# First MLP's down projection as 16 pairs of seven-product blocks, rows finished by accumulating transfers, first key and query products in row groups

## The chip, the core and the metric

The kernel runs on one core of a Trainium2 chip. The metric is device time in microseconds (us) of one execution; the time before is the median of three runs. The profile is of one more execution of the same program. TensorE is PE in the profile, VectorE is DVE, ScalarE is ACT, GpSimd is POOL, SyncE is SP.

## The reference: what is computed

A trunk of two layers works on 1024 prompt tokens and 8 sample tokens, so on T = 1032 columns of width 1024. Layer 0 mixes tokens with a recurrent block, layer 1 with sliding-window attention; after each mixer comes a squared-ReLU MLP. All is float32.

```python
def sq_relu_mlp(x, w_up, w_down):
    return jnp.square(jax.nn.relu(x @ w_up)) @ w_down      # 1024 -> 4096 -> 1024

yp = yp + mp                                               # mixer's output
yp = yp + sq_relu_mlp(rms_norm(yp, norm_mlp_g[layer]), w_up[layer], w_down[layer])
# layer 1 then begins with
h = rms_norm(yp, norm_mix_g[1]); q, k, v = split(h @ w_qkv); q, k normed per head
```

The change lies at the end of layer 0's MLP and at the beginning of layer 1's attention.

## The kernel before, in words

**Number format.** Each float32 operand is split into a high part (`hi`, rounded by an ACT cast) and a low part (`lo`, what is left, by a DVE subtraction). A product is three passes: hi·hi, hi·lo, lo·hi, that is three matmuls for each block of 128 rows of the contraction.

**Seven-product blocks.** The two MLPs are computed in the manner of Strassen and Winograd. Two 128-row tiles of the hidden width are a pair (16 pairs in all), and two 128-row tiles of the output are a block `q`. A block takes seven products (`i` = 1 to 7 in `BY`) of sums of weight quarters (`S1` to `S4`, built by DVE) with sums of token halves (`B11`, `T1` and so on). A product of one pair is three matmuls of 512 columns (i = 1, 2, 4) or six of 260 (i = 3, 5, 6, 7). The contraction is over several pairs at once, a chunk. `steady` writes the order of the products by hand: within a block 1, 6, 2, 7, 4, 5, 3, with the next block's product 1 before this block's product 3; in the last block (`FINAL`) 1, 6, 7, 4, 5, 2, 3. `e` and `o` are the two rows of output tiles of a block; product 5 completes `o`, and product 3 is accumulated in the same PSUM tile (`z["d"]`) after DVE has read product 5 out of it, and completes `e`.

**Down projection of layer 0.** The up projection writes the sums of the hidden tokens to DRAM (`hsum`). The down projection runs over chunks of pairs; for each chunk it makes four blocks (eight output rows), loading `tl` tiles from `hsum` and splitting them (ACT L467, DVE L468). Before, layer 0 has 14 pairs in this form, in chunks of 3, 3, 3, 3 and 2. Finished rows of the first four chunks are added to the residual in DRAM by an accumulating transfer of POOL (L773: `acc[m] += t`). For the last chunk, the transfer goes the other way (L782: `t += acc[m]`), and the row stays in SBUF. The other two pairs are four plain hidden tiles (`hid`, `hdh`/`hdl`), and `down_steps` multiplies them in the ordinary way: for each third of the columns (344 columns) and each of eight rows twelve matmuls, then DVE adds the product to the row (L384), ACT squares it for the norm (L290) and makes `hh` (L390), DVE makes `hl` (L391). After each third the squares of eight rows, summed by DVE, go through a matmul with ones (L302, `tokens`). Layer 1's down projection has all 16 pairs as blocks, in chunks of 4, 3, 3, 3 and 3.

**First products of the attention.** `proj_many` makes the first key and first query tile (`k0`, `q0`) third by third: 24 matmuls of a key third, 24 of a query third. Each key third is then normed by a serial chain: ACT squares it (L851) and copies it (L852), a matmul with the head mask sums the squares (L858), DVE and ACT find the factor (L859, L314 to L316, L317, L319), DVE multiplies (L926), and ACT and DVE split the result (L869, L870). There is one PSUM bank for the sums (`bN`). `proj_steps` then makes the second key tile (`k1`, 72 matmuls, L943), with three such chains more. `v_proj` (216 matmuls of 256 columns, L973) accumulates four pairs of token blocks in two banks (`bS`), and the eight samples in `bT`. ACT reads these banks out (L983), with a scale per token `rt`, which `by_token` issues behind the last key chain. After that comes the second query tile.

**What sets the order.** The code is written in program order, and a scheduler then moves instructions in each engine's queue by priority and by its estimate of when they are ready; on the chip every queue runs in its order. Loads of weights pass through two `raw` tiles of the pool `rp` (SP issues them), and a `raw` tile comes free when ACT and DVE have split it (L183, L184).

Of the kernel before, what the change touches and what calls it, by code (L numbers as in the profile page):

```python
# [16 lines left out]
P = 128  # L17
# [13 lines left out]
CHUNKS = [[range(0, 3), range(3, 6), range(6, 9), range(9, 12), range(12, 14)],  # L31
          [range(0, 4), range(4, 7), range(7, 10), range(10, 13), range(13, 16)]]
NSP = [c[-1][-1] + 1 for c in CHUNKS]
RQ = [6 * P, 8 * P]
NRAW = [4, 3]
# [30 lines left out]
def trunk(ctx: ExitStack, tc: tile.TileContext, I, O):  # L66
# [103 lines left out]
    def fetch(n):  # L170
        while len(raws) < min(n, len(units)):
            name, _, src, _ = units[len(raws)]
            if name[:2] == "dn":
                raws.append(small["pool"].tile([P, RQ[int(name[2])]], F32, tag="Q", name=nm("raw")))
            else:
                raws.append(R("raw"))
            sp.dma_start(raws[-1][:, 0:src.shape[1]], src)
# [23 lines left out]
    for layer in range(2):  # L201
        add_units(f"up{layer}", I["w_up"][layer], 2 * NPAIR, lambda j: None)
        for b in range(4 * len(CHUNKS[layer])):
            for j in range(2):
                units.append((f"dn{layer}", 2 * b + j, I[f"w_dn{layer}"][2 * b + j][:, 0:2 * P * len(CHUNKS[layer][b // 4])], None))
# [8 lines left out]
    def ensure(k):  # L214
        while nloaded[0] <= min(k, len(units) - 1):
            n, j, _, alloc = units[nloaded[0]]
            fetch(nloaded[0] + (NRAW[int(n[2])] if n[:2] == "dn" else 2))
# [131 lines left out]
    def tokens(ssq, c):  # L349
# [4 lines left out]
        ssq.total(ps)  # L354
# [17 lines left out]

    def down_steps(w, srcs, xs, gname, hs, after=None, col=lambda m, k: k * P, early=0):
        for c in range(NCH):
            ssq = SumSq(plain=True)
            held = []
            if c == 0 and early:
                held = banks3("P")
                for m in range(3):
                    yield from mm_steps([held[m]], w(m), srcs, [c], col=lambda k: col(m, k), ks=range(early))  # L380
            for m in range(M8):
                o, ks = (held[m], range(early, len(srcs))) if m < len(held) else (B("P" if held and m == 3 else None)[:, :CH], None)
                yield from mm_steps([o], w(m), srcs, [c], col=lambda k: col(m, k), ks=ks)
                dve.tensor_tensor(xs[m][:, cs(c)], o, xs[m][:, cs(c)], ALU.add)  # L384
                if after:
                    after(m, c)
                x, (hi, lo), g = xs[m][:, cs(c)], hs[m], V(gname, m)
                with tc.high_priority():
                    ssq.add(x, m)
                act.activation(r_(hi[:, cs(c)]), x, AF.Copy, scale=g)  # L390
                dve.scalar_tensor_tensor(r_(lo[:, cs(c)]), x, g, hi[:, cs(c)], ALU.mult, ALU.subtract)  # L391
            if c == 0:
                last["c0"] = last["sq"]
            tokens(ssq, c)

# [74 lines left out]
    class TokenOps:  # L472
# [43 lines left out]
        def T1(self, e, o, j):  # L516
# [6 lines left out]
    LAST = {"tile": (24, 25, 26, 27), "split tile": (28, 31, 34, 38),  # L523
            "weights": (14, 15, 23, 24), "split weights": (19, 22, 53)}
# [19 lines left out]
    PROGS = [UP + steady("dn", range(4 * len(c))) for c in CHUNKS]  # L544
# [4 lines left out]
    class PairWeights:  # L549
        def __init__(self, layer):  # L550
            self.layer = layer
            self.prog, self.chunks = PROGS[layer], CHUNKS[layer]
# [83 lines left out]
    class Ahead:  # L636
        def __init__(self, layer):
            self.sums = hsum[layer]
            self.chunks = CHUNKS[layer]
# [3 lines left out]
            self.pooled = layer  # L643
            self.lag = {0: 4, 1: 4} if layer else {0: 4}
# [7 lines left out]
        def split(self, step):  # L652
            with tc.issue_after(last["copy"]):
                while self.raw and self.raw[0][0] <= step - self.lag.get(self.raw[0][1], 5):
                    _, c, name, t = self.raw.pop(0)
                    pooled = self.pooled and c == 0 and len(self.ops[c][name]) in ()
                    self.ops[c][name].append(op_at(*t, pool if pooled else dve))
# [24 lines left out]
    xd = []  # L682

    def mlp_products(layer, tok, pw, r, spill, acc, gnext, after):
        ahead = Ahead(layer)
        chunks, nsp = CHUNKS[layer], NSP[layer]
        final = None if gnext else 4 * len(chunks) - 1
        hs, raw = [], []
        ws, wraw = [], []
        xs = xd  # L690
        xs[:] = [None] * M8
# [5 lines left out]
        def last_tile(k):  # L697
            lo, hi = A("hdl"), A("hdh")
            pool.dma_start(lo, hid[layer][k])
            return hi, lo  # L700

        def last_weights(j):
            t = R("raw")
            sp.dma_start(t[:, 0:D], I[f"w_dn{layer}"][8 * len(chunks) + j])
            return t

        for n, (kind, q, i) in enumerate(PROGS[layer]):
# [7 lines left out]
            if (kind, q, i) == ("up", NU, 4):  # L715
                swap_small(f"q{layer}", NRAW[layer])
            wt = pw.take(n)
            first = up and q < 2
            if i == 1:
                st[q] = {"z": ZB(), "e": spare("he") if not up and q in range(2 if gnext else 1, 12 if gnext else final - 1) else A("he"), "o": A("ho")}  # L720
# [12 lines left out]
            with tc.high_priority():  # L733
                if i == 1:
                    last["copy"] = act.copy(e0, d).ins  # L735
                elif i == 6 and not first:
# [4 lines left out]
                    if not up and q == final:  # L741
# [10 lines left out]
                elif i == 2 and not first:  # L752
                    last["copy"] = act.copy(e0, d).ins  # L753
                    if not up and q == final:
# [8 lines left out]
            for ready in done:  # L763
                t = z[ready]
                if up:
                    dve.scalar_tensor_tensor(t, t, 0.0, r, ALU.min, ALU.mult)
                    act.activation(t, t, AF.Square)
                    if q >= nsp:
                        act.dma_start(hid[layer][2 * (q - nsp) + (ready == "o")], t)
# [4 lines left out]
                elif q == final:  # L774
# [6 lines left out]
                else:  # L781
                    pool.dma_start(t, acc[m], accum_op=ALU.add)  # L782
# [4 lines left out]
            if "e" in done:  # L787
                if up and q < nsp:
# [9 lines left out]
            elif not up:  # L798
                c, k = divmod(n - NUP, 28)
                ahead.split(n)  # L800
                if final:
# [22 lines left out]
        if final:  # L824
            return
# [826 lines left out]
```

## Time and profile before

| | |
|---|---|
| median of 3 runs | 1953.07 us (1952.73 to 1954.8) |
| profiled execution | 1954.17 us, of which the span from the first to the last instruction is 1952.4 us |
| PE, PEld, DVE, ACT, POOL busy | 99%, 93%, 76%, 52%, 18% of the span |
| down blocks of layer 0 (14 pairs) | 649.03 to 928.27 us |
| `down_steps` | 928.27 to 975.39 us |
| first key product to the first matmul of the second query tile | 975.39 to 1040.56 us |
| down blocks of layer 1 (16 pairs) | 1628.82 to 1947.03 us |

The stages are read from the timeline of PE: the start of the first matmul of each. Busy shares of matmuls are modelled, and a matmul's own duration (282 ns for one of 260 columns) overlaps its neighbours', so the pitch of matmuls is taken from start to start.

### The profile page before, as it was taken

The page shows a single profiled execution, that of the slowest core. Times are in us where ns is not written, and L with a number is a line of the kernel's source. Part 1 is how long each engine was busy: PE and PEld are TensorE (multiplying, and loading weights), DVE is VectorE, ACT ScalarE, POOL GpSimd, SP SyncE. Part 2 cuts the span into 40 slices and gives each one's busy share as a digit, 9 for nine tenths or more (in the row PEclk, how much of TensorE's full clock was granted, in tenths as well). Part 3 has the DMA queues.
Part 4 walks back from the last instruction along what each step waited for, and adds up shares of the span by engine and source line. Part 5 has one row for each costly group of instructions (what it writes and reads, how often), then busy time and mean ns, then how long its engine had stood idle before and what let it go on. Part 6 is the DMA issues. An engine that isn't in the chain of part 4 may idle for free.

```text
span 1952.4 us, 34246 instructions
## 1 busy us (share of the span) xinstructions
PE 1939.8 (99%) x12844; PEld 1806.6 (93%) x12844; DVE 1477.1 (76%) x2715; ACT 1007.5 (52%) x1993; POOL 359.0 (18%) x699
## 2 busy tenths in 40 slices
PE   9999999999999999999999999999999999999998
PEld 9999999999999899999999887999999999999998
DVE  7996747987777888778753778589877779687884
ACT  6585635443434655455554667465444436455552
POOL 1320000000000232322022667000000003223221
PEclk9999999999999999999999999999999999999999
DMA  5111242244445788888453336622443447788877
GB/s 188 40 45 54 80 156 84 100 162 158 142 158 175 230 223 240 215 198 209 137 150 91 110 101 203 211 84 99 163 145 138 163 166 261 211 196 218 237 193 181
DMA packets 115909, 308.17 MB, mean 158 GB/s; under 512 B 17560, under 2 KB 46240, under 8 KB 115744
## 3 DMA queue, kind: packets, MB, share of 16 engines
q0 software_dynamic: 30720, 104.18, 22.2%
q1 hardware_dynamic: 56800, 131.45, 20.5%
q10 hardware_dynamic: 28224, 70.35, 10.0%
q8 instruction: 101, 1.65, 0.4%
q14 instruction: 64, 0.52, 0.1%
HBM read 178.08 MB, written 115.16 MB: 150 GB/s over the span
## 4 chain that ended last, share of the span: by engine, by line
PE 93%; DVE 3%; ACT 2%; issue 1%; DMA 1%; POOL 0%; SPq 0%; DVEq 0%; ACTq 0%
PE bD L613 36%; PE bZ L613 26%; PE bP L244 12%; PE bS L244 7%; PE bT L244 3%; PE bP L943 3%; PE bO L1084 1%; PE bSS L1037 1%; PE bS L973 1%; PE bT L1064 1%; ACT se L1050 1%; DVE op L461 1%; DMA x<-spill 0%; DMA raw<-w_in 0%; DVE wl L184 0%
## 5 line engine op out<-in xcount | busy, mean ns | idle before, releaser
L613 PEld LDWEIGHTS bD<-op,op 128*128 128x128 f32 x3072 | 380.6, 188 | 7.9
L613 PE MATMUL bD<-op,op 128*128 128x260 f32 x3072 | 383.2, 282 | 0.0
L613 PEld LDWEIGHTS bD<-tl,op 128*128 128x128 f32 x2880 | 362.2, 188 | 11.8 <-DVE ho L761 0.3
L613 PE MATMUL bD<-tl,op 128*128 128x260 f32 x2880 | 366.2, 282 | 0.1
L626 POOL DMA_DIRECT2D tl<-hsum x210 | 125.2, 682 | 884.5 <-PE bD L613 783.5
L460 ACT CAST op<-ws 128x512 fp32r<-128x512 f32 (+2 forms) x288 | 158.4, 560 | 248.4 <-DVE ws L581 124.6
L613 PE MATMUL bZ<-op,op 128*128 128x512 f32 x1152 | 282.3, 395 | 0.0
L613 PE MATMUL bZ<-tl,op 128*128 128x512 f32 x1080 | 271.9, 395 | 0.2 <-DVE tl L468 0.2
L613 PEld LDWEIGHTS bZ<-op,op 128*128 128x128 f32 x1152 | 210.5, 188 | 43.9 <-ACT he L747 0.2
L613 PEld LDWEIGHTS bZ<-tl,op 128*128 128x128 f32 x1080 | 194.3, 188 | 37.7 <-DVE tl L468 0.7
L468 DVE TENSOR_TENSOR tl<-tl 128x520 fp32r<-128x520 f32 (+1 forms) x210 | 136.6, 692 | 77.0 <-ACT tl L467 76.9
L460 ACT CAST op<-raw 128x512 fp32r<-128x512 f32 (+2 forms) x216 | 120.8, 561 | 139.1 <-PE bD L613 76.5
L461 DVE TENSOR_TENSOR op<-ws,op 128x512 fp32r<-128x512 f32 (+2 forms) x288 | 171.5, 610 | 8.7 <-ACT op L460 8.5
L461 DVE TENSOR_TENSOR op<-raw,op 128x512 fp32r<-128x512 f32 (+2 forms) x216 | 131.5, 610 | 5.4 <-ACT op L460 4.5
L761 DVE TENSOR_TENSOR ho<-bD,ho 128x520 f32<-128x520 f32 x140 | 97.5, 696 | 37.4 <-PE bD L613 35.0
L467 ACT CAST tl<-tl 128x520 fp32r<-128x520 f32 (+1 forms) x210 | 117.7, 626 | 2.4 <-DMA tl<-hsum 1.0
L184 DVE TENSOR_TENSOR wl<-raw,wh 128x512 fp32r<-128x512 f32 (+1 forms) x76 | 65.7, 885 | 37.6 <-ACT wh L183 20.8
L751 DVE TENSOR_TENSOR ho<-bZ,ho 128x512 f32<-128x512 f32 x72 | 49.5, 687 | 43.7 <-PE bZ L613 43.3
L761 DVE TENSOR_TENSOR he<-bD,he 128x520 f32<-128x520 f32 x71 | 49.4, 696 | 40.9 <-PE bD L613 40.4
L753 ACT COPY he<-bZ 128x512 f32<-128x512 f32 x68 | 39.9, 587 | 78.0 <-PE bZ L613 65.6
L183 ACT CAST wh<-raw 128x512 fp32r<-128x512 f32 (+1 forms) x76 | 56.9, 775 | 41.9 <-PE bT L244 13.9
L735 ACT COPY he<-bZ 128x512 f32<-128x512 f32 x72 | 42.0, 583 | 70.4 <-PE bZ L613 70.3
(371 smaller groups left out, 3811.5 us busy)
## 6 DMA issues: line engine op xcount, KB each, us to landing
raw<-w_up SPq DMA_DIRECT2D x64, 512.0 KB, 3.9
tl<-hsum POOLq DMA_DIRECT2D x120, 260.0 KB, 6.8
raw<-w_dn SPq DMA_DIRECT2D x64, 384.0 KB, 6.2
tl<-hsum POOLq DMA_DIRECT2D x90, 256.0 KB, 6.7
spill<-ho POOLq DMA_DIRECT2D x32, 516.0 KB, 6.8
spill<-he POOLq DMA_DIRECT2D x32, 516.0 KB, 6.2
hsum<-ts ACTq DMA_DIRECT2D x30, 520.0 KB, 4.0
hsum<-ho ACTq DMA_DIRECT2D x30, 516.0 KB, 3.6
```

What stands on the lines that cost most here:

```text
L183: act.copy(r_(hi[:, sl]), raw[:, sl])
L184: eng.tensor_tensor(r_(lo[:, sl]), raw[:, sl], hi[:, sl], ALU.subtract)
L244: pe.matmul(o, lhsT=r_(wt[:, col(k):col(k) + P]), rhs=r_(xt[:, cs(c)]), start=(k == first and a == 0), stop=(k == final and a == 2))
L460: act.copy(r_(hi), x)
L461: dve.tensor_tensor(r_(lo), x, hi, ALU.subtract)
L467: act.copy(r_(hi), lo)
L468: eng.tensor_tensor(r_(lo), lo, hi, ALU.subtract)
L613: pe.matmul(d[:, 512 * b:512 * b + c], lhsT=r_(wt[:, j * P:j * P + P]), rhs=r_(xt[:, c * b:c * b + c]), start=first and j == 0 and a == 0, ...
L626: pool.dma_start(t[:, n:2 * n], src)
L751: dve.tensor_tensor(o0, d, o[:, HP], ALU.add)
L761: last["sum"] = dve.tensor_tensor(t, inner(d), t, ALU.add).ins
L943: pe.matmul(o, lhsT=r_(wt[:, k * P:k * P + P]), rhs=r_(xt[:, cs(c)]), start=(k == 0 and a == 0), stop=(k == M8 - 1 and a == 2))
```

## The change

Layer 0 gets layer 1's plan: all 16 pairs as blocks, chunks of 4, 3, 3, 3 and 3, and three `raw` tiles of down weights in place of four. `down_steps`, the four plain tiles and their weights are gone. The eight rows of the last chunk are finished by accumulating transfers, the last `e` row in two parts. As each row lands, `row(m)` squares it over all 1032 columns (ACT), makes `hh` (ACT) and `hl` (DVE), adds the square to one running sum (DVE) and stores the row (SP). The first key and query products then hold six banks at once and take the rows in three groups: rows 0 to 3, rows 4 and 5, rows 6 and 7. The three matmuls with ones stand between the products of the second group. The six results are read out after the third group.

```diff
-CHUNKS = [[range(0, 3), range(3, 6), range(6, 9), range(9, 12), range(12, 14)],
-          [range(0, 4), range(4, 7), range(7, 10), range(10, 13), range(13, 16)]]
-NRAW = [4, 3]
+CHUNKS = [range(0, 4), range(4, 7), range(7, 10), range(10, 13), range(13, 16)]
+NRAW = 3
...
-    def mlp_products(layer, tok, pw, r, spill, acc, gnext, after):
+    def mlp_products(layer, tok, pw, r, acc, gnext, store):
...
+        def row(m):
+            x, g, s, hi, lo = xs.pop(m), V(gnext, m), A("sq"), A("hh"), A("hl")
+            act.activation(s, x, AF.Square)
+            act.activation(r_(hi), x, AF.Copy, scale=g)
+            sp.dma_start(store[m], x)
+            if sq:
+                dve.tensor_tensor(sq[0], sq[0], s, ALU.add)
+            else:
+                sq.append(s)
+            dve.scalar_tensor_tensor(r_(lo), x, g, hi, ALU.mult, ALU.subtract)
+            hn[m] = (hi, lo)
...
                 elif i == 2 and not first:
                     last["copy"] = act.copy(e0, d).ins
-                    if not up and q == final:
+                    if not up and q == final and gnext:
+                        pool.dma_start(e0, acc[2 * (q % 4)][:, H0], accum_op=ALU.add)
+                    elif not up and q == final:
...
                 else:
-                    pool.dma_start(t, acc[m], accum_op=ALU.add)
+                    sl = slice(HW if q == final and ready == "e" else 0, T)
+                    pool.dma_start(t[:, sl], acc[m][:, sl], accum_op=ALU.add)
...
+                if gnext and c == len(chunks) - 1:
+                    m = 2 * (q % 4) - 2
+                    if i == 7 and m >= 0:
+                        row(m + 1)
+                    if i == 5 and m >= 0:
+                        row(m)
+                    if q == final and i in (2, 5):
+                        ensure(index["k" if i == 2 else "q", 0])
...
-        ws += [split_unit(t, W, dve) for t in wraw]
-        hn = [(A("hh"), A("hl")) for _ in range(M8)] if gnext else None
-        run(down_steps(lambda m: ws, hs, xs, gnext, hn, after=after, col=lambda m, k: m * P, early=2))
-        return hn
+        row(7)
+        row(6)
+        rs["sq"] = sq[0]
+        return [hn[m] for m in range(M8)]
...
-        with tc.issue_after(last["c0"]):
-            wk, wq = unit("k", 0, 1), unit("q", 0, 1)
-        proj_many([wk, wq], hs, lambda i, c, o: q_evac(0, c, o) if i else k_evac(0, c, take_out(o), fx["row"][:, cs(c)]))
+        ws = [unit("k", 0, 0), unit("q", 0, 0)]
+        firsts = [(i, c, B()[:, :CH]) for c in range(NCH) for i in range(2)]
+        for rows in (range(0, 4), range(4, 6), range(6, 8)):
+            for i, c, o in firsts:
+                mm_group([o], ws[i], hs, [c], ks=rows)
+                if rows[-1] == 5 and i:
+                    tokens(rs["sq"][:, cs(c)], c)
+        for i, c, o in firsts:
+            if i:
+                q_evac(0, c, o)
+            else:
+                k_evac(0, c, take_out(o), fx["row"][:, cs(c)])
         run(proj_steps(unit("k", 1, 1), lambda c, o: k_evac(1, c, take_out(o), fx["row"][:, cs(c)]), iter(())))
         by_token()
         v_proj()
```

Three places in the built programs show how queues change. The same code has lower line numbers in the changed kernel: L582 for L613, L715 and L727 for L751 and L761, L819 for L858, L934 for L973.

The first is DVE at the last block of the down projection. Before, after the last product's reading the queue goes on with `down_steps`:

```order
L761 TENSOR_TENSOR ho_9744<-bD_9798,ho_9744 128x520
L751 TENSOR_TENSOR ho_9744<-bZ_9818,ho_9744 128x512
L761 TENSOR_TENSOR ho_9744<-bD_9826,ho_9744 128x520
L761 TENSOR_TENSOR he_9743<-bD_9826,he_9743 128x520
L384 TENSOR_TENSOR he_9377<-bP_9894,he_9377 128x344
```

Now the sum of squares and the low half of row 4 (`sq_10170`, `he_9870`, the row of the block before) stand between the last block's own readings (`ho_10035`, `he_10034`):

```order
L665 TENSOR_TENSOR sq_9813<-sq_9813,sq_10170 128x1032
L715 TENSOR_TENSOR ho_10035<-bZ_10138,ho_10035 128x512
L668 SCALAR_TENSOR_TENSOR hl_10172<-he_9870,vec,hh_10171 128x1032
L727 TENSOR_TENSOR ho_10035<-bD_10149,ho_10035 128x520
L725 TENSOR_TENSOR he_10034<-bD_10149,he_10034 128x260 x2
```

The reading of product 5 (`L727 ho_10035`), which the last product waits for, has moved behind two instructions that wait for a row in flight.

The second is ACT between the first key third's square and the second's. Before (`wh` casts split weights; `bP_10438` and `bS_10530` are key thirds):

```order
L851 ACTIVATE sq_10463<-bP_10438 128x344
L852 COPY x_10464<-bP_10438 128x344
L314 ACTIVATE q_10475<-sq_10463,st 128x344
L315 ACTIVATE r_10474<-q_10475 128x344
L316 ACTIVATE q_10475<-r_10474 128x344
L881 ACTIVATE sq_10520<-bS_10493 128x344
L183 CAST wh_10708<-raw_10430 128x512
L869 CAST hi_10482<-x_10464 128x344
L883 CAST hi_10522<-bS_10493 128x344
L183 CAST wh_10708<-raw_10430 128x512
L183 CAST wh_10886<-raw_10706 128x512 x2
L851 ACTIVATE sq_10555<-bS_10530 128x344
```

Now, from the first third's logarithm on (`bP_10276` is the second key third; `raw_10571` and `raw_10749` are the second value tile's and the second query tile's weights):

```order
L311 ACTIVATE q_10457<-sq_10445,st 128x344
L312 ACTIVATE r_10456<-q_10457 128x344
L180 CAST wh_10751<-raw_10571 128x512
L313 ACTIVATE q_10457<-r_10456 128x344
L180 CAST wh_10751<-raw_10571 128x512
L180 CAST wh_10759<-raw_10749 128x512 x2
L830 CAST hi_10464<-x_10446 128x344
L844 CAST hi_10479<-bP_10275 128x344
L812 ACTIVATE sq_10487<-bP_10276 128x344
```

Four casts of newly loaded weights have moved into the first chain, and the second key third's square stands behind the end of that chain.

The third is PE around the sixth and last key norm (`bN`). Before, it stands in the middle of the first value bank's 48 products:

```order
L973 MATMUL bS_10900<-wh_10886,hh_9892 128x256
L973 MATMUL bS_10900<-wl_10887,hh_9892 128x256
L973 MATMUL bS_10900<-wh_10886,hl_9893 128x256
L858 MATMUL bN_10849<-sq_10845,con 128x344
L973 MATMUL bS_10900<-wh_10708,hh_9878 128x256
```

Now the samples' 24 products (`bT`) follow the first two value banks, and the norm stands among them; `bS_10867` is the third value bank, which takes the place of the first:

```order
L934 MATMUL bT_10972<-wl_10752,hh_10131 8x256
L819 MATMUL bN_10714<-sq_10710,con 128x344
L934 MATMUL bT_10972<-wh_10751,hl_10132 8x256
L934 MATMUL bT_10972<-wh_10751,hh_10241 8x256
L934 MATMUL bT_10972<-wl_10752,hh_10241 8x256
L934 MATMUL bT_10972<-wh_10751,hl_10242 8x256
L934 MATMUL bT_10972<-wh_10751,hh_10233 8x256
L934 MATMUL bT_10972<-wl_10752,hh_10233 8x256
L934 MATMUL bT_10972<-wh_10751,hl_10234 8x256
L934 MATMUL bS_10867<-wh_10573,hh_9862 128x256
```

Between the last norm and the third value bank stand now 7 products, where before stood 72.

More of the change, by code (lines that the diff above doesn't have):

```diff
@@ L353, in tokens @@
         ps = B("N")[:, :CH]
-        ssq.total(ps)
+        pe.matmul(ps, lhsT=ones, rhs=sq, start=True, stop=True)
         act.copy(row[:, cs(c)], ps)
@@ L695, in spare @@
             return R(s)
[L697 to L707, printed above, removed]
+        def row(m):
[9 more added lines that the diff above has]
+            hn[m] = (hi, lo)
+        for n, (kind, q, i) in enumerate(PROG):
             up = kind == "up"
@@ L800, in mlp_products @@
                 ahead.split(n)
[L801 removed]
+                if True:
                     if c == 0 and k in NEXT:
@@ L1498, in ahead, with mlp @@
         return f
-    def mlp(layer, r, spill, gnext, after):
+    def mlp(layer, r, acc, gnext, store):
         swap_banks(f"pu{layer}")
-        return mlp_products(layer, rs.pop("tok"), rs.pop(layer), r, None, spill, gnext, after)
+        return mlp_products(layer, rs.pop("tok"), rs.pop(layer), r, acc, gnext, store)
     r0 = A("rt")
```

101 lines of the change are left out of this document (26 added, 75 removed).

## The prediction, made before the run

> **What bounds the kernel.** I read the page first.
>
> ```profile
> span 1952.4 us, 34246 instructions
> ...
> PE 1939.8 (99%) x12844; PEld 1806.6 (93%) x12844; DVE 1477.1 (76%) x2715; ACT 1007.5 (52%) x1993; POOL 359.0 (18%) x699
> ```
>
> PE bounds it, and hardly ever stands still. So the change is worth what it takes from PE's products, less each new pause of PE. The waits of PE say how little there is now:
>
> ```profile
> PE bO L1084 <- DVE pt L1068: 1.5, 1, 1.5
> ```
>
> That is the longest of all (total, times, longest, in us). Then the table of stretches, for the two down projections and what lies around:
>
> ```profile
> core 0: us, PE busy (x) PEld busy (x) DVE busy (x) ACT busy (x) POOL busy (x), PEclk, DMA share, GB/s
> 649.03:928.27 279.24, 279.01 (x1850) 255.65 (x1849) 225.20 (x427) 150.26 (x293) 77.27 (x118) 1.00 0.83 213
> 928.27:975.39 47.12, 47.12 (x295) 46.20 (x293) 35.59 (x71) 25.66 (x53) 0.88 (x1) 1.00 0.46 132
> 975.39:1040.56 65.17, 64.86 (x448) 61.40 (x447) 27.72 (x57) 30.31 (x70) 14.84 (x29) 1.00 0.48 133
> 1628.82:1947.03 318.21, 318.12 (x2114) 292.10 (x2112) 241.30 (x444) 156.74 (x299) 86.07 (x135) 1.00 0.80 207
> ```
>
> These are layer 0's 14 pairs, `down_steps`, the first key, query and value products, and layer 1's 16 pairs. In each PE is busy nearly all the time.
>
> **Part 1: the products, a gain.** Layer 0 takes on the plan that layer 1 runs already, so the price of 16 pairs stands in the last row: 318.21 us. It replaces 279.24 + 47.12 = 326.36: **-8.15 us**. Of this 1.4 us is no gain, as two matmuls with ones move from `down_steps` into the next stage; I count them there. A check by matmuls:
>
> ```profile
> 1940.47 2.32 PE L613 MATMUL bD<-tl,op 128*128 128x260 f32 x18
> 1942.63 2.25 PE L613 MATMUL bZ<-tl,op 128*128 128x512 f32 x9
> 1944.71 2.32 PE L613 MATMUL bD<-tl,op 128*128 128x260 f32 x18
> ```
>
> ```profile
> 928.43 13.27 PE bP L244 x84
> ...
> 977.92 0.70 PE bN L302 x2
> ```
>
> From start to start a matmul of 260 columns takes 2.16/18 = 0.120 us, one of 512 takes 2.08/9 = 0.231, one of 344 takes 13.27/84 = 0.158. Out go 288 of 344 columns, 45.5 us; in come 2 pairs x 4 blocks x (24 of 260, 9 of 512), 39.7 us: -5.8. The stages give -8.15 + 1.4 = -6.75, as layer 0's blocks run 0.06 us a pair slower than layer 1's. I take the stages and keep -5.8 for the upper end. The other additions (two pairs' sums stored, 14 more `tl` loads, wider weights) hide as in layer 1, whose stretch pauses for 0.1 us.
>
> **Part 2: the finishing of rows, a loss in the last blocks.** `row` puts, per row, two ACT instructions of 1032 columns and two DVE instructions into blocks 17 to 19. In layer 1 nothing of this kind stands there. The prices:
>
> ```profile
> L467 ACT CAST hdh<-hdl x4: 1056/1057/1057, 889.9 to 903.6; 128x1032 fp32r<-128x1032 f32 x4
> L468 DVE TENSOR_TENSOR hdl<-hdl,hdh x4: 1222/1222/1224, 891.0 to 905.0; 128x1032 fp32r<-128x1032 f32 x4
> ```
>
> ```profile
> 924.96 0.69 DVE L751 TENSOR_TENSOR ho<-bZ,ho 128x512 f32<-128x512 f32 x1
> 925.76 0.70 DVE L761 TENSOR_TENSOR ho<-bD,ho 128x520 f32<-128x520 f32 x1
> 928.47 0.70 DVE L761 TENSOR_TENSOR he<-bD,he 128x520 f32<-128x520 f32 x1 [2.01 <-PE bD L613]
> ```
>
> ```profile
> 929.68 0.88 POOL L782 DMA_DIRECT2D he<-spill  x1 [1.84 <-issue]
> ```
>
> ```profile
> DMA to landing us min/median/max: 5.4/6.0/7.2
> ```
>
> The last is the accumulating transfer of a finished row in layer 0. Follow row 4 from the end of block 18's last product. DVE completes it at 0.2 to 0.9; POOL issues at 1.4 (929.68 against 928.47, 1.2 us later); it lands at 7.4; ACT squares it to 8.5. DVE's queue holds the sum of squares there, and behind it, in order, the reading of product 4, row 4's low half, and the reading of product 5: 8.5 + 1.22 + 0.69 + 1.22 + 0.70 = 12.3. The last product accumulates onto product 5's bank, so PE must wait for this; its own five products before end at 3 x 2.16 + 2 x 2.08 = 10.6. PE waits **1.7 us** (1.1 to 2.9 for the landing's ends). Blocks 17 and 18 have the same order with one more product as cover, but also build the next block's weights; I put 0.4 us on each, between 0 and 1 (an estimate from the same rows). Together **+2.5 us**, with ends 0.5 and 5.
>
> Rows 6 and 7 themselves are covered. The last part of row 6 is complete 0.8 us after the last product and lands by about 8; square, sum, high and low halves are done by 12. PE has 72 + 12 matmuls, 13.3 us, before the first matmul with ones, and 19 us before it needs the row.
>
> **Part 3: the key norms, the larger loss.** Before, each of the first three norms stood behind a query third, and its chain ran beside products. Now all six banks end together, so the first chain begins when the last product of `k0` and `q0` is done. A chain step is serial, and this is what the chain of waits shows from one norm to the next:
>
> ```profile
> 1011.47 0.86 PE bN L858 x2
> ...
> 1016.79 0.46 ACT sq L851
> ...
> 1017.29 0.84 PE bN L858 x2
> 1018.14 19.80 PE bS L973 x168
> ```
>
> One norm follows another after 5.82 us at best, because ACT's queue takes the next square only behind the split of this key. A product of 256 columns takes 19.80/168 = 0.118 us. Behind the last norm comes:
>
> ```profile
> 1023.37 0.30 ACT L314 ACTIVATE q<-st,vec 128x9 f32<-128x9 f32 x1 [0.26 <-DMA kh<-hi]
> ...
> 1024.72 0.84 ACT L983 ACTIVATE vt<-bS,st 128x256 f32<-128x256 f32 x2 [0.56 <-DVE st L319]
> ```
>
> Only 1025.56 - 1017.29 = 8.27 us after the last norm is the first value bank free, and PE needs that bank for the third one. Now PE's walk, from the end of the last down product:
> - 144 matmuls of `k0` and `q0` x 0.158 + 3 with ones x 0.70: 24.85. First norm 0.84 and a third of `k1` (24 x 0.158): 29.5. Then the queue holds the second norm.
> - Its square stands behind casts of four weight halves, and those of the value tile wait for a transfer:
>
> ```profile
> raw<-w_qkv SPq DMA_DIRECT2D x8, 512.0 KB, 4.2
> ```
>
> ```profile
> 985.51 0.48 ACT L869 CAST hi<-x 128x344 fp32r<-128x344 f32 x1
> 985.90 0.44 ACT L883 CAST hi<-bS 128x344 fp32r<-128x344 f32 x1
> 986.24 1.66 ACT L183 CAST wh<-raw 128x512 fp32r<-128x512 f32 x3
> ```
>
> ```profile
> 983.74 0.58 DVE L317 SCALAR_TENSOR_TENSOR q<-sq,st,q 128x344 f32<-128x344 f32 x1 [1.70 <-ACT q L316]
> 984.35 0.52 DVE L319 SCALAR_TENSOR_TENSOR r<-q,r 128x344 f32<-128x344 f32 x1
> 984.90 0.58 DVE L926 SCALAR_TENSOR_TENSOR x<-x,qg,r 128x344 f32<-128x344 f32 x1
> 985.61 0.69 DVE L184 TENSOR_TENSOR wl<-raw,wh 128x512 fp32r<-128x512 f32 x1
> ```
>
>   The `raw` tile comes free when `k1`'s weights are split: first query bank done at 21.1, square 0.5, two casts 0.55 each, a low half 0.7, so 23.4. The load lands 4.2 later, the cast ends at 28.2. What is left of the first chain is ACT's last square, 0.5, DVE's three steps with two low halves between them, 0.6 + 0.7 + 0.5 + 0.7 + 0.6, and the split of the key, the split of the query third and the square of the next key, 0.5 + 0.4 + 0.5: about 33.1. PE waits **3.6 us**. Without the casts the square would come at 31.1 and PE wait 1.6: the lower end.
> - From 33.1: norms three, four and five come at 39.5, 46.1 and 51.9, where PE's own work (24 + 11 matmuls; 13 + 31; 41) and the chain's steps end within 0.2 us of each other. The last norm is at 57.7.
> - Seven products later PE needs a value bank: 8.27 - 0.84 - 7 x 0.118 = **6.6 us** of waiting, to 66.0. Before, 72 products (8.5 us) stood there. The remaining 96 end at 77.3.
>
> The stretch took 65.17: **+12.1 us**, of which 10.2 are the two waits. Behind PE in these waits stand only its own products; ACT and DVE are the ones waited for.
>
> All stretches above have PEclk 1.00, and no pause exceeds 1.5 us, so no row shows a clock after a long pause. [...]
>
> **Sum.** -8.15 + 2.5 + 12.1 = +6.45 us. The profiled execution took 1954.17, so it would take 1960.6; it lies 1.1 above the median of 1953.07, and I forecast against the median: **1959.5 us**.
>
> **Rivals.**
> - *The chains are covered after all.* If the value banks were read out within 1.7 us of the last norm and no norm were late, only the products would change: -6.5, 1946.6 us. For it: PE paused 0.31 us in this stretch. Against it: the idle time before `vt` ended with DVE's `st`, the chain's end, and 65 products have left the place behind the last norm. It decides if the waits together stay under 2.6 us. Chance 0.06.
> - *Waits shorter than worked out.* Second norm at 31.1, rows landing in 5.4 us: +2.5 to 3.5, about 1956, within 0.2%. Chance 0.20.
> - *Rows land late.* In layer 1 the same transfers took longer:
>
> ```profile
> DMA to landing us min/median/max: 6.5/7.3/9.1
> ```
>
>   Each us beyond 6.0 delays the last product by as much; 9.1 costs 3.1 more, 1962.6. From 11 us on the matmuls with ones wait too. Chance 0.12.
> - *PE slows after a pause.* A pause of 6.6 us is four times the longest here. If products behind it ran at half pace for as long as the shorter wait, 3.6 us, 1.8 us would be lost for each wait: 1961.3 to 1963.1. [...] Chance 0.17.
>
> **How the numbers follow.** The forecast has 0.45, with its own range 1957 to 1962. Lower end for all terms: 0.5 in part 2 and a second norm at 31.1 give +2.45; upper end: 5 in part 2, 0.9 for the smaller gain of products, give +9.9, and with a slower PE 13.3. The range is 1954 to 1965; out of it fall the first rival and the tails, some 0.16. About 0.2% (3.9 us) is what a measurement can tell from no change: faster 0.06, same 0.20, slower 0.74.
>
> **What the changed profile would show.** Right: layer 0's blocks take 318 to 323 us; a wait of PE at L582 for DVE L727 of 1 to 3 us; a wait at L819 for ACT's square of 2 to 4 us; a wait at L934 `bS` for ACT's `vt` near 6.6 us. Wrong: no wait above 2 us between the last down product and the second query tile, or PE pausing before the matmuls with ones (L351), which would say that rows land later than 11 us.

## The result, and the profile after

The changed kernel takes 1970.4 us (median of 4 runs, 1968.5 to 1971.1) against 1953.7 us for the kernel before on the same chip: a ratio of 1.0084, 95% interval 1.0066 to 1.0101, so 16.7 us slower. The forecast was 1959.5, 6.45 us slower: the right direction, and less than half of the size.

The page first, span and busy time of the engines:

```profile
span 1968.6 us, 34123 instructions
...
PE 1940.5 (99%) x12820; PEld 1803.2 (92%) x12820; DVE 1476.9 (75%) x2680; ACT 1006.3 (51%) x1967; POOL 365.5 (19%) x710
```

PE has 24 matmuls less than before and is "busy" 0.7 us longer. Fewer products that take longer: a hint that some of them ran slowly. The waits of PE (total, times, longest, in us) are those that the prediction named, in the places it named:

```profile
PE bD L582 <- DVE ho L727: 6.6, 3, 4.5
PE bS L934 <- ACT vt L944: 6.3, 1, 6.3
PE bN L819 <- ACT sq L812: 3.4, 2, 3.1
```

The table of stretches: the 16 pairs of layer 0 (start of the first `tl` product to the first key product), the first attention products (to the second query tile), then four short pieces:

```profile
core 0: us, PE busy (x) PEld busy (x) DVE busy (x) ACT busy (x) POOL busy (x), PEclk, DMA share, GB/s
649.33:976.91 327.58, 320.88 (x2114) 293.87 (x2113) 253.59 (x456) 170.48 (x315) 84.49 (x130) 0.99 0.78 205
976.91:1058.12 81.21, 71.40 (x451) 67.34 (x451) 31.50 (x59) 33.06 (x71) 15.71 (x30) 0.91 0.45 121
955.20:970.00 14.80, 13.09 (x90) 11.93 (x90) 7.71 (x11) 4.59 (x5) 1.74 (x2) 1.00 0.79 212
973.00:978.00 5.00, 5.00 (x23) 5.00 (x24) 0.77 (x2) 0.00 (x0) 1.77 (x2) 0.52 0.65 102
1009.30:1013.00 3.70, 3.69 (x11) 3.22 (x12) 0.80 (x2) 1.76 (x4) 2.11 (x4) 0.50 0.71 186
1044.00:1048.00 4.00, 3.57 (x16) 3.57 (x17) 0.00 (x0) 1.11 (x4) 1.18 (x3) 0.50 0.64 154
```

The column PEclk was 1.00 in every stretch quoted of before. Here it stands at about 0.5 in three pieces, and each of them lies right behind one of PE's three long pauses (start, duration, in brackets the idle time before and who ended it):

```profile
972.85 4.27 PE L582 MATMUL bD<-tl,op 128*128 128x260 f32 x18 [4.51 <-DVE ho L727]
...
1009.31 1.51 PE L819 MATMUL bN<-sq,con 128*128 128x344 f32 x2 [3.08 <-ACT sq L812]
...
1044.43 0.58 PE L934 MATMUL bS<-wh,hh 128*128 128x256 f32 x1 [6.29 <-ACT vt L944]
```

The 18 matmuls of the first row took 4.27 us; 18 of the same form took 2.32 before. The pause of 1.3 us that ended at 955.25 left the clock at 1.00.

Why the first pause is 4.5 us long shows in the rows of block 19. Row 4's transfer is issued by POOL at 958.92, beside two weight loads that SP has just issued, and ACT can square the row only at 968.05, 9.1 us later:

```profile
956.42 1.54 SPq L174 DMA_DIRECT2D raw<-w_qkv  x2
```

```profile
958.92 0.87 POOL L747 DMA_DIRECT2D he<-spill  x1 [2.35 <-DVE he L702]
```

```profile
968.05 1.06 ACT L661 ACTIVATE sq<-he 128x1032 f32<-128x1032 f32 x1 [1.52 <-DMA he<-spill]
```

On DVE's queue the sum of that square stands ahead of the reading that PE's last product waits for (972.10):

```profile
969.15 1.23 DVE L665 TENSOR_TENSOR sq<-sq,sq 128x1032 f32<-128x1032 f32 x1 [1.11 <-ACT sq L661]
970.30 0.68 DVE L715 TENSOR_TENSOR ho<-bZ,ho 128x512 f32<-128x512 f32 x1
970.90 1.28 DVE L668 SCALAR_TENSOR_TENSOR hl<-he,vec,hh 128x1032 fp32r<-128x1032 f32 x1
972.10 0.69 DVE L727 TENSOR_TENSOR ho<-bD,ho 128x520 f32<-128x520 f32 x1
```

### The profile page after: what moved, and what is told of

It reads as the page before. It is cut to its first block, busy times and chain, and to the rows that moved or that the text cites. A ratio compares the mean times of both kernels' runs of the same rounds, so it can differ in the third digit from the quotient of the medians.

```text
span 1968.6 us, 34123 instructions
## 1 busy us (share of the span) xinstructions
PE 1940.5 (99%) x12820; PEld 1803.2 (92%) x12820; DVE 1476.9 (75%) x2680; ACT 1006.3 (51%) x1967; POOL 365.5 (19%) x710
## 4 chain that ended last, share of the span: by engine, by line
PE 45%; DVE 3%; ACT 1%; DMA 1%; issue 1%; POOL 0%; DVEq 0%; SPq 0%; ACTq 0%
PE bD L582 18%; PE bZ L582 13%; PE bP L904 3%; PE bP L241 3%; PE bS L241 2%; PE bS L934 1%; PE bO L1045 1%; PE bSS L998 1%; PE bT L241 1%; ACT se L1011 1%; PE bT L1025 1%; DVE op L432 1%; DMA he<-spill 0%; DMA x<-spill 0%; PE bN L819 0%
## 5 line engine op out<-in xcount | busy, mean ns | idle before, releaser
L582 PEld LDWEIGHTS bD<-tl,op 128*128 128x128 f32 x3072 | 386.8, 189 | 19.4 <-DVE ho L727 8.5
L582 PE MATMUL bD<-tl,op 128*128 128x260 f32 x3072 | 391.2, 283 | 6.8 <-DVE ho L727 6.6
L582 PEld LDWEIGHTS bD<-op,op 128*128 128x128 f32 x3072 | 380.4, 188 | 7.8
L582 PE MATMUL bD<-op,op 128*128 128x260 f32 x3072 | 382.9, 282 | 0.0
L431 ACT CAST op<-ws 128x512 fp32r<-128x512 f32 (+1 forms) x288 | 162.0, 572 | 255.2 <-DVE ws L550 127.7
L582 PE MATMUL bZ<-tl,op 128*128 128x512 f32 x1152 | 288.1, 394 | 0.0
L582 PE MATMUL bZ<-op,op 128*128 128x512 f32 x1152 | 282.2, 395 | 0.0
L582 PEld LDWEIGHTS bZ<-op,op 128*128 128x128 f32 x1152 | 210.5, 188 | 43.9 <-ACT he L711 0.2
L582 PEld LDWEIGHTS bZ<-tl,op 128*128 128x128 f32 x1152 | 207.9, 188 | 40.3 <-DVE tl L439 0.4
L439 DVE TENSOR_TENSOR tl<-tl 128x520 fp32r<-128x520 f32 (+1 forms) x224 | 145.4, 692 | 75.7 <-ACT tl L438 75.7
L431 ACT CAST op<-raw 128x512 fp32r<-128x512 f32 (+1 forms) x216 | 123.4, 573 | 146.2 <-PE bD L582 83.1
L432 DVE TENSOR_TENSOR op<-ws,op 128x512 fp32r<-128x512 f32 (+1 forms) x288 | 176.4, 627 | 8.7 <-ACT op L431 8.5
L432 DVE TENSOR_TENSOR op<-raw,op 128x512 fp32r<-128x512 f32 (+1 forms) x216 | 135.1, 627 | 7.5 <-ACT op L431 6.7
L727 DVE TENSOR_TENSOR ho<-bD,ho 128x520 f32<-128x520 f32 x140 | 97.6, 697 | 36.7 <-PE bD L582 35.2
L715 DVE TENSOR_TENSOR ho<-bZ,ho 128x512 f32<-128x512 f32 x72 | 49.6, 689 | 43.8 <-PE bZ L582 43.5
L727 DVE TENSOR_TENSOR he<-bD,he 128x520 f32<-128x520 f32 x70 | 48.8, 697 | 37.6 <-PE bD L582 37.4
L1011 ACT ACTIVATE se<-se,den,st 128x129 f32<-128x129 f32 x128 | 61.8, 486 | 21.7 <-DVE den L1008 20.6
```

What stands on the lines that cost most here:

```text
L431: act.copy(r_(hi), x)
L432: dve.tensor_tensor(r_(lo), x, hi, ALU.subtract)
L439: eng.tensor_tensor(r_(lo), lo, hi, ALU.subtract)
L582: pe.matmul(d[:, 512 * b:512 * b + c], lhsT=r_(wt[:, j * P:j * P + P]), rhs=r_(xt[:, c * b:c * b + c]), start=first and j == 0 and a == 0, ...
L715: dve.tensor_tensor(o0, d, o[:, HP], ALU.add)
L727: last["sum"] = dve.tensor_tensor(t, inner(d), t, ALU.add).ins
```

## The experiments

The theory to be tested: the excess over the forecast is (a) a late row ahead of a wanted reading in DVE's queue and (b) some 2 us at half rate behind each of the three long pauses. All times are medians; "before" was run again beside each and lay between 1953.3 and 1953.7.

**1. Read rows 5 and 4 out later.**

```diff
-                    if i == 7 and m >= 0:
+                    if q < final and i == 7 and m >= 0:
...
-        row(7)
-        row(6)
+        with tc.issue_after(last["read"]):
+            for m in (5, 4, 7, 6):
+                row(m)
```

`last["read"]` is DVE's last reading of the last product.

> The reading out of rows 5 and 4 (squares, scaled halves, DVE's sums) is queued behind DVE's last reading of the last down product; the accumulating transfers start as before. Theory (in the kernel after, DVE reads the row that lands 9.1 us late ahead of the sum that PE's last product waits for; the 4.5 us pause and about 2.1 us of slow clock behind it follow from that): the pause in block 19 goes, 1970.4 - 6.6 = about 1964, up to 1967 if rows 4 to 7 now come late for the second or third row group. Rival (the rows themselves are late for everything behind them, so the wait only moves to the first key and query products): 1969 to 1971.

Measured: 1962.45 us, 1.0045 (1.0031 to 1.0058): 7.9 less than the kernel after. The waits of PE between 640 and 1130 us are now:

```profile
PE bS L935 <- ACT vt L945: 6.3, 1, 6.3
PE bN L820 <- ACT sq L813: 3.6, 3, 3.2
PE bD L582 <- DVE ho L727: 1.9, 2, 1.2
```

The pause in block 19 is gone and has not reappeared: the rows still land nearly as late (ACT waits for row 5 until 962.95, against 963.89 in the kernel after), but nothing that PE needs soon stands behind them. The order on DVE's queue was the cost. The rival falls. Of the 7.9 us, 4.5 were the pause and 2.5 the half rate behind it. The loss by half rate behind the second norm, at which the edit did not aim, also fell from 3.0 to 1.7 us (see the last section).

**2. Read each key bank out right behind its own last row group.** The loop over the third group also calls `k_evac` and `q_evac`.

```diff
-        for rows in (range(0, 4), range(4, 6), range(6, 8)):
+        for rows in (range(0, 4), range(4, 6)):
...
         for i, c, o in firsts:
+            mm_group([o], ws[i], hs, [c], ks=range(6, 8))
             if i:
                 q_evac(0, c, o)
```

> Each bank of the first key and query products is read out right behind its own third row group, in program order, so that the first norm sum stands about 27 products (4.2 us) earlier on PE's queue. Theory (the norm chains start too late, each of PE's two waits, 3.1 and 6.3 us, is followed by about 5 us of half rate, 2.1 to 2.6 us lost each): the first chain ends about 4 us earlier, the 3.1 us wait and its slow clock go, the 6.3 us wait falls to 2 to 4 us: 1962 to 1965. Rival (the chains are set by their own length on ScalarE and VectorE, one behind the other, not by PE's order): 1969 to 1971.

Measured: 1970.07 us, 1.0083 (1.0069 to 1.0097): nothing. A miss. The first norm does come earlier on PE, at 996.98 instead of 1001.71, and the second at 1004.76 instead of 1009.31. But the third waits for its square:

```profile
1015.00 1.51 PE L819 MATMUL bN<-sq,con 128*128 128x344 f32 x2 [3.37 <-ACT sq L812]
```

So the wait moved from the second norm to the third, and the value bank came free no sooner (a wait of 6.2 us). An earlier place on PE's queue does not shorten a chain of ACT and DVE steps.

**3. Both edits together.**

> The two edits above together. Theory: the savings add up, 1955 to 1959. Rival (with the pause in block 19 gone, the rows or the chains come late by the same amount further on): 1963 or more.

Measured: 1961.53 us, 1.0041 (1.0028 to 1.0055). That is the first edit's gain and no more, as experiment 2 leaves one to expect.

**4. Undo the row groups.** The key and query products go back to the order of before (token sums first, whole products after); the new down projection stays.

```diff
-        firsts = [(i, c, B()[:, :CH]) for c in range(NCH) for i in range(2)]
-        for rows in (range(0, 4), range(4, 6), range(6, 8)):
...
+        for c in range(NCH):
+            tokens(rs["sq"][:, cs(c)], c)
+        proj_many(ws, hs, lambda i, c, o: q_evac(0, c, o) if i else k_evac(0, c, take_out(o), fx["row"][:, cs(c)]))
```

> The first key and query products as in the kernel before (token sums first, then whole products), the down projection and the rows' finishing as in the kernel after. Theory (the row groups cost the two norm waits of 3.1 and 6.3 us and 4.7 us of slow clock, and save a wait for rows 6 and 7): the norm waits go, -14 us, and PE waits for the last row's square instead, 977 to 985.5 us, 8.5 us and some 2.4 us of slow clock: about 1967. Rival (the time was lost in the down projection, and the norm waits are covered elsewhere): no saving, the new wait on top, 1977 to 1981.

Measured: 1962.2 us (1960.8 to 1967.6), 1.0053 (1.0041 to 1.0066), 8.2 less than after. The second norm and the third value bank no longer keep PE waiting (0.3 us is the longest wait for a norm). The waits at L582 are those of the kernel after; the second line, for the last row, is new:

```profile
PE bD L582 <- DVE ho L727: 6.7, 3, 4.4
PE bP L241 <- ACT hh L662: 2.7, 1, 2.7
```

The direction of the theory holds; the price of the new wait was put too high (8.5 us), since the scheduler let 31 products of the first thirds run ahead of the token sums.

**5. The row groups alone, on the kernel before.** The reverse test of part 3.

> The kernel before, with nothing but the first key and query products taken in row groups (rows 0 to 3, 4 and 5, 6 and 7 over six banks), as in the kernel after; the down projection and the rows are those of before. Theory (the row groups alone cost the key norms' waits, 3.1 and 6.3 us, and two times 2.3 us at half rate): about 1953.7 + 14 = 1968, 1964 to 1969. Rival (the norm chains run late only behind the late rows of the new down projection): 1954 to 1957.

Measured: 1965.42 us, 1.0059 (1.0045 to 1.0073): 12.0 slower than before. The same two waits (the norm's longest, 3.2 us, and the value bank's) stand there, with no late row and none of the new down projection:

```profile
PE bS L973 <- ACT vt L983: 6.1, 1, 6.1
PE bN L858 <- ACT sq L851: 4.2, 3, 3.2
```

That shows that the norm waits come from the row groups, not from late rows. The 12.0 lie a little under the 14 expected, within the range given.

**6. Keep PE at work through a pause.** Thirty products more, in a bank that nobody reads, in the 6.3 us ahead of the third value block.

```diff
+            for b2 in (0, 1, "t", "f", 2, 3):
...
+                if b2 == "f":
+                    spare_bank = B("O")[:, :CH]
+                    with tc.issue_after(last["bt"]):
+                        for n in range(30):
+                            pe.matmul(spare_bank, lhsT=r_(w[0][0][:, 0:P]), rhs=r_(hs[0][0][:, 0:CH]), start=True, stop=True)
...
+                    continue
```

The edit also writes the samples' products (`"t"`) ahead of the fill; in the kernel after the scheduler had already put them there.

> The kernel after, with 30 products of 344 columns more (4.7 us, into a bank that nobody reads) between the samples' value products and the value bank that waits: PE works through most of its 6.3 us wait, and the wait ends when it did. Theory (a pause of over some 3 us costs about 5 us at half rate): the value products behind it run at 0.118 us each from the start, -2.1 to -2.6 us, 1967.8 to 1968.3 against 1970.4. Rival (the slow products come from something else, such as the operands or the banks): no change or up to 1 us slower.

Measured: 1966.83 us (1964.7 to 1970.1), 1.0067 (1.0054 to 1.0079): 3.5 less, from a kernel that does more. The scatter is so large that the time alone does not settle it; the profile does. The first row is the 4 us behind the wait in the kernel after, the second the same place here:

```profile
1044.43:1048.40 3.97, 3.97 (x18) 3.97 (x19) 0.00 (x0) 0.68 (x2) 0.75 (x2) 0.50 0.57 138
```

```profile
1043.17:1047.00 3.83, 3.83 (x32) 3.83 (x33) 0.00 (x0) 0.68 (x2) 0.76 (x2) 1.00 0.58 142
```

Here 1.5 us of pause were left, the clock stayed at 1.00, and 32 matmuls fall into the time that held 18. The slow products come from the pause, not from their operands or banks. The profile is of the slowest execution (1970.1). By the wait for `pt` in the attention it was 3.4 us ahead of the kernel after (1199.13 against 1202.55), and it lost that again by a pause of 1.85 us that ended at 1214.93 and the half rate behind it (PEclk 0.67 over 1214 to 1218); why this pause came was not followed.

**7. Hold the weight loads back.** The loads of the second key tile and the first value tile are queued on SP behind row 4's store.

```diff
                     if q == final and i in (2, 5):
-                        ensure(index["k" if i == 2 else "q", 0])
+                        with tc.issue_after(last["store"]):
+                            ensure(index["k" if i == 2 else "q", 0])
```

> The kernel after, with the 512 KB loads of the second key unit and the first value unit queued behind row 4's store on SP, so that they no longer run beside the accumulating transfers of rows 5 and 4. Theory (those loads make the rows land after 9 us instead of the stage's median of 6.4 us): row 4's square starts 2.5 us earlier, the pause of 4.5 us falls under 3 us with no slow clock behind it: 1964 to 1966. Rival (the landing time is the accumulating transfer's own, or the other row's beside it): 1969 to 1971.

Measured: 1964.03 us, 1.0051 (1.0038 to 1.0063): 6.3 less than after. Landing times of the accumulating transfers of the stage, in the kernel after and here:

```profile
DMA to landing us min/median/max: 4.8/6.4/9.0
```

```profile
DMA to landing us min/median/max: 5.3/5.8/7.1
```

ACT squares row 4 at 964.10, 5.7 us after POOL's issue at 958.44. The last product waits 1.0 us, and no half rate follows: 3.5 us of pause and 2.5 us of slow clock are gone, about the 6.3 us measured. The close fit is in part chance, since half rate also stayed away behind the second norm here and came at another place (see the last section). So what made the row late were the two loads beside it: a landing of 5.7 us is within the ends that the prediction took from before (5.4 to 7.2).

**8. Take the value wait away.** On top of experiment 1, the third value block goes to a bank that is free there.

```diff
-                ps = B("S")
+                ps = B("O" if b2 == 2 else "S")
```

> On top of the later reading out of rows 5 and 4 (1962.45): the third value block's products go to bank O, which is free there, in place of the second of the two S banks, so that PE's 48 products of 0.118 us (5.7 us) no longer wait for ScalarE to empty a bank behind the last key norm. Theory (the 6.3 us wait and some 2.4 us of slow clock behind it are real time on the path): 0.6 us of wait left, 1962.45 - 5.7 - 2.4 = about 1954.5. Rival (the attention behind it waits for the same chain of norms and factors, so the time comes back as another wait): 1960 to 1963.

Measured: 1956.45 us, 1.0013 (1.0004 to 1.0022): 6.0 of the 8 us, but not all by the way that was foreseen. The value wait fell only from 6.3 to 3.8 us, since the fourth block needs an S bank too:

```profile
PE bS L935 <- ACT vt L945: 3.8, 1, 3.8
PE bN L820 <- ACT sq L813: 1.5, 2, 0.8
```

The second line shows the rest: the free bank let the scheduler put 27 products of the third block ahead of the second norm, so that its wait of 3.2 us and the 1.7 us of half rate behind it went too. The square that this norm needs came no sooner (1001.50, against 1001.19 in experiment 1). PE had other work.

**9. Copy the key banks out one chain earlier as well.**

```diff
+        outs = {}
         for i, c, o in firsts:
...
+            for a in range(c, min(c + 2, NCH)):
+                if a not in outs:
+                    outs[a] = take_out(firsts[2 * a][2])
-                k_evac(0, c, take_out(o), fx["row"][:, cs(c)])
+            k_evac(0, c, outs[c], fx["row"][:, cs(c)])
```

> As the run before, and the first key's banks are copied out one norm chain earlier (ScalarE's square and copy of bank c+1 ahead of chain c), so that the second norm sum no longer waits for a square behind the first chain. Theory: the 3.2 us wait and about 2.3 us of slow clock go too: about 1949, faster than the kernel before (1953.5). Rival (each chain's own length decides, PE only waits later, at the second query unit or the value banks): 1953 to 1955.

Measured: 1959.8 us, 1.003 (1.0019 to 1.0042), 3.4 worse than without it. A miss again. The fourth norm now waits 3.3 us, and the value wait has grown to 4.2:

```profile
PE bS L935 <- ACT vt L945: 4.2, 1, 4.2
PE bN L820 <- ACT sq L813: 3.3, 1, 3.3
```

In the timeline of ACT a key's split waits for a transfer out of the small tile that it is to write:

```profile
1024.02 0.48 ACT L831 CAST hi<-x 128x344 fp32r<-128x344 f32 x1 [2.74 <-DMA kh<-hi]
```

It may be that early copies hold more of the nine small tiles, so that the chains run into each other. That is not shown: experiment 1 has a wait of 2.3 us of this kind without them.

**10. A bank for each value block.** Experiment 8, with the fourth block in a P bank.

```diff
-                ps = B("O" if b2 == 2 else "S")
+                ps = B(("S", "S", "O", "P")[b2])
```

> As the run with the third value block in bank O (1956.45), and the fourth block in a P bank, so that no value block waits for a bank that ScalarE empties behind the last key norm. Theory: the 3.85 us wait and some 2.2 us at half rate go, and PE runs on into the second query unit while the chains end: about 1950.4, faster than the kernel before (1953.7). Rival (the second query unit or the attention waits for the same chains): 1954 to 1957.

Measured: 1952.18 us, 0.9993 (0.9984 to 1.0002): level with the kernel before, 1.8 more than forecast. The long waits are gone; PE runs on while the chains end. The waits for norms grew from 1.5 to 2.0 us:

```profile
PE bN L820 <- ACT sq L813: 2.0, 2, 1.4
PE bD L582 <- DVE ho L727: 1.9, 2, 1.2
```

**11. Read rows 0 and 2 out behind their block.**

```diff
-                    if q < final and i == 5 and m >= 0:
+                    if final - 3 < q < final and i == 3:
                         row(m)
```

> As the run with four banks for the value blocks (1952.18), and the reading out of rows 0 and 2 queued behind the last product of blocks 17 and 18, so that VectorE's row work no longer stands ahead of the sums that PE's products wait for there. Theory (the pauses of 0.8 and 1.2 us left in these blocks are VectorE's row work in its queue): they go, 1952.2 - 1.9 = about 1950.3, faster than the kernel before by 0.15%. Rival (VectorE's other work in the blocks, the splits of the operands, takes the place): 1952.

Measured: 1949.19 us, 0.9978 (0.9969 to 0.9987). The pauses in blocks 17 and 18 are gone, and the waits for norms fell from 2.0 to 1.4 us. This version beats both kernels: 4.1 us under before and some 21 under after, with all three parts of the change in it. Its two stages, to be held against the first two rows of the table of the kernel after:

```profile
648.54:967.07 318.53, 318.45 (x2114) 292.27 (x2113) 248.82 (x452) 169.72 (x315) 84.49 (x130) 1.00 0.80 211
967.07:1035.49 68.42, 66.18 (x453) 62.44 (x451) 34.83 (x61) 33.81 (x74) 15.72 (x30) 1.00 0.53 140
```

## Why the prediction was right in direction and wrong in size

Experiment 11 issues the same products in its first stage (2114), with no pause there. Its two stages less their pauses are taken as the bare price of the work, so each term can be sized:

| term of the sum | forecast | measured | how |
|---|---|---|---|
| part 1, products | -8.15 | -7.8 | 318.53 - 326.36 |
| part 2, pauses in blocks 17 to 19 | +2.5 | +6.6 | 0.8 + 1.3 + 4.5 |
| half rate behind block 19's pause | none | +2.4 | 327.58 - 318.53 - 6.6 |
| part 3, two norm waits | +10.2 | +9.7 | 3.4 + 6.3 |
| half rate behind them | none | +5.2 | 81.21 - 9.7 - (68.42 - 2.1) |
| part 3, the rest | +1.9 | +1.1 | 68.42 - 2.1 - 65.17 |
| all | +6.45 | +17.2 | |

The 2.1 us are the pauses left in experiment 11's second stage (1.4 at the norms and 0.7 ahead of the second query tile). The two profiled spans differ by 16.2: the changed kernel enters the first stage 0.3 us later and gets 1.4 us back behind the second. The half rate can also be read from the trace: it lasted 4.9, 6.0 and 5.0 us from the ends of the three pauses (972.85 to 977.77, 1009.31 to 1015.32, 1044.43 to 1049.45), half of which is 2.5, 3.0 and 2.5 us, 8.0 together against 7.6 in the table. Of the four signs that the prediction gave for being right, two came (3.1 us at L819, 6.3 us at L934) and two did not (layer 0's blocks took 327.6 us, and the wait at L582 was 4.5 us).

- **Part 1** held within 0.4 us. Layer 1's stretch was the right row to price layer 0's new plan by.
- **Part 2, the landing of row 4, is one step that failed.** The place, the order on DVE's queue and the arithmetic were right: with 9.1 us in place of 6.0 the working gives 1.7 + 3.1 = 4.8 us, and 4.5 was measured. The 6.0 was the median of eight transfers. In their stretch such a pair of 512 KB loads stands too, from 922.53 on, and the transfer then in flight (issued at 921.16) was the slowest of the eight, at 7.2. In the changed kernel the two loads start just ahead of row 4's transfer (`ensure` at products 2 and 5 of the last block); the diff shows the line, and the sum put them at nothing. Experiment 7 showed the price: 3.5 us of pause, and 2.5 us of slow clock behind it. The 0.4 us put on each of blocks 17 and 18 were 0.8 and 1.3.
- **The sum left the clock out; that is the other step.** The 4.5 us, 3.1 us and 6.3 us pauses were each followed by half rate, worth 7.6 us together. The prediction had this as a rival (0.17), for two pauses, at half pace for 3.6 us each, which makes 1.8 us; no row of before showed a clock behind a long pause, so pace and length were assumed. It was three pauses, with half rate (PEclk 0.50) for 4.9 to 6.0 us behind each and 2.5 to 3.0 us lost. Experiment 6 shows that the pause brings it: with 1.5 us of it left in place of 6.3, the clock was 1.00 in place of 0.50. The length of a pause alone does not tell whether half rate follows, as the last section shows.
- **Part 3's waits** came out as worked out: 3.1 for 3.6 us and 6.3 for 6.6. The order on ACT and DVE was the one foreseen, but the transfer of weights held the casts up for only 0.41 us. Experiments 4 and 5 show that the waits come from the row groups, and experiments 8 and 10 that the value wait is one for a bank.
- **How the rivals were used is the third fault.** "Rows land late" (+3.1) and "PE slows after a pause" were given as alternatives. Both can come true, and the first feeds the second, since the late row makes a third long pause: 1959.5 + 3.1 + 7.6 = 1970.2, against 1970.4 measured. So close a fit is luck, as blocks 17 and 18 cost 1.3 us more than forecast and part 3 without its slow clock 1.3 us less. The prediction's own upper end did hold both (+13.3, which is 1966.4), with 3.4 us for the slow clock, but the range was closed below it, at 1965. No run shows these 3.4 us; the runs showed 7.6 in their place.

## What to carry to other kernels

When a change puts new reading-out work on an in-order queue, look at what stands behind it: here the order was worth 7 to 8 us, and putting the late reader last cost no new wait. Price a transfer with what will run beside it after the change, not with its median before (here 9.1 us with two loads beside it, 5.7 without). Behind the pauses of PE of 1.85 to 6.3 us that were followed here stood, besides their own length, 1.4 to 3.1 us lost by slow products (nothing behind one of 3.26 us), so such a pause is worth a spare bank or a few products from elsewhere. A bank that is free early pays twice, as in experiment 8: it ends its own wait and gives the scheduler work for another. Rivals that can both come true have to be added up too.

## What the runs showed of the hardware

Half rate did not come behind every long pause. In the kernel after, the clock is 0.50 over 970.94 to 977.77, 1008.49 to 1015.32 and 1042.62 to 1049.45, so from before the end of each pause. Each of the three stretches is 6.83 us long, twice 3.41, and their starts lie 37.55 and 34.13 us apart, 11 and 10 times 3.413. Experiments 1 and 7 have nearly the same pause at the second norm, 3.18 and 3.26 us (columns as above, the granted clock third from the end). In experiment 1 PE was busy for 1.34 us of the 3.42 us that hold most of the pause, and the next 3.41 us ran at half rate:

```profile
999.62:1003.04 3.42, 1.34 (x7) 1.14 (x8) 2.75 (x6) 1.64 (x5) 0.95 (x2) 1.00 0.66 195
1003.04:1006.45 3.41, 3.41 (x14) 3.41 (x14) 1.65 (x4) 1.56 (x3) 1.16 (x3) 0.50 0.89 245
```

In experiment 7 the pause lies across two stretches of this length, with 1.57 and 2.00 us of work in them, and no half rate followed:

```profile
998.53:1001.94 3.41, 1.57 (x10) 1.28 (x9) 3.24 (x6) 2.08 (x5) 0.00 (x0) 1.00 0.31 80
1001.94:1005.35 3.41, 2.00 (x11) 1.80 (x12) 2.20 (x5) 2.03 (x5) 1.61 (x4) 1.00 0.73 207
1005.35:1008.77 3.42, 3.42 (x24) 3.42 (x23) 1.67 (x3) 1.11 (x4) 0.51 (x1) 1.00 0.75 235
```

In the attention of experiment 7 two pauses of 0.81 and 0.84 us fell into 3.41 us, and half rate followed:

```profile
1203.33:1206.74 3.41, 1.76 (x15) 0.88 (x12) 3.31 (x8) 3.28 (x11) 0.80 (x2) 1.00 0.95 332
1206.74:1210.15 3.41, 3.41 (x16) 3.35 (x15) 2.87 (x6) 2.10 (x10) 3.23 (x8) 0.50 1.00 344
```

So the length of a pause does not decide alone: 3.26 us were followed by full clock, two pauses of under 0.9 us by half rate, and so was the one of 1.85 us in experiment 6. Nor does PE's work in the 3.41 us ahead order these rows: half rate followed on 1.34 and 1.76 us of it, and not on 1.57 (busy times rest on modelled ends of matmuls). What decides is not shown. What is lost is half of the time that PE works at half rate: 2.5, 3.0 and 2.5 us behind the three pauses of the kernel after, 3.1 behind the third norm in experiment 2 (1015.00 to 1021.2), 1.7 behind the second norm in experiment 1, where the 3.41 us at 0.50 were filled with work, and 1.4 behind the value wait in experiment 7 (1036.65 to 1039.5). As no run shows how to choose where half rate falls, part of each time here may be luck.
